# Value-scale squares, gate row and forget sums take other places in a hybrid attention layer

## The chip, the cores and the metric

The kernel runs on one core of a Trainium2 chip. The metric is the time of one execution on the device in microseconds (us). A run gives one time; where a median is named, it is over the runs shown. Engines are named PE (TensorE, with PEld for its weight loads), DVE (VectorE), ACT (ScalarE), POOL (GpSimd) and SP (SyncE, which here only issues DMAs). Line numbers with an L are those of the kernel before, unless the text says that they are of the changed one.

## What is computed

One residual sub-layer over 1024 tokens of width 1024, all in float32. The input is normalised and modulated (u), projected once to queries, keys, values and gates of 16 heads (and 8 columns for forget gates); eight heads do stick-breaking attention and eight do softmax attention with a cumulative forget gate; both are gated by SiLU, projected, multiplied by a modulation gate, added to the input and normalised. The reference, cut:

```python
mod = jax.nn.silu(c) @ w_ada[layer] + b_ada[layer]
shift, scale, gate = ...                       # three parts of 1024
u = layer_norm(x) * (1.0 + scale) + shift
fq, fk, fv, fg, ff, sq, sk, sv, sg = _split_columns(u @ w_in[layer])
log_f = log_sigmoid(ff + b_f)
f_cum = jnp.cumsum(log_f, axis=1)

# softmax heads
s = q @ k.T * scale + (f_q[..., :, None] - f_k[..., None, :])
p = softmax(where(causal, s, -inf));  out = p @ v

# stick-breaking heads
z = q @ k.T * scale
log_keep = where(strict, log_sigmoid(-z), 0.0)
later = cumsum(log_keep, axis=3, reverse=True) - log_keep
w = where(strict, exp(log_sigmoid(z) + later), 0.0);  out = w @ v

y = concat([y_fox * silu(fg), y_sb * silu(sg)]) @ w_out
x = layer_norm(DEEPNORM_ALPHA * x + gate * y, ln_g, ln_b)
```

Three small results matter here. The **value scales**: for pairs 2 to 7 the weights and values are kept as float16 parts, and the values are scaled by a factor that is worked out on the chip from the sum of squares of the value weights of their group. The **gate row**: gate = silu(c) @ w_ada, one row of 1024 numbers. The **forget sums**: the running sum of log_f over the 1024 tokens.

## The kernel before, in words

**Pairs and units.** Two heads share 128 partitions, so there are eight head pairs, four stick-breaking (0 to 3), then four softmax (4 to 7). A unit (p, h, i) is one block of 128 queries of head h of pair p against the i+1 blocks of keys up to it; there are 16 units to a pair, and `order(p)` says in which order. A step k of the main loop at the end of the program takes one unit's scores (`scores_turn`) and the weights of the unit two steps earlier for pairs 0 and 1, five steps earlier later (`weights_turn`).

**A stick-breaking unit** (`att_scores`, L598 on). PE computes the scores S into two PSUM banks (L611 and L613: high and low part of the keys). ACT reads them twice with a sigmoid: kp (L646) and be (L648). DVE runs a scan over kp from the right (L654, and L658 for the second half where the keys do not fit in 512 columns); in the program this is `tensor_tensor_scan`, and the order listing below names it SCALAR_TENSOR_TENSOR. POOL multiplies be by the scanned kp (L660). For pairs 0 and 1 PE then transposes the product in blocks of 128 into a PSUM buffer called T (L691, `att_transpose`); ACT copies it to the high part of pt and DVE subtracts to get the low part (L694), which frees the T buffer. There are two T buffers. Pairs 2 and 3 transpose by DMA instead. PE multiplies by the values into the "value bank" pv (`att_pv`, L720 for pairs 0 and 1, L709 later), whose columns 256 to 511 are idle for pairs 2 and on. ACT, DVE (L739, L740) and POOL (L741) turn it into a slice of y (tile ty).

**Projections as fillers.** Between the steps PE does matmuls of the later pairs' projections (L329 to L331 for q, k and g, L441 to L443 for values). They come from generators that are chained in `fillers`, near the end; each `yield` is one step, and `fill(want)` says how many steps stand behind each unit (52 in pair 0, 72 in pair 1). `beside(main, sides)` advances its side generators once with each step of its main one, and a `for _ in range(N): yield` in a side generator sets how many main steps it lets pass. The side generators are `gen_gate` (gate row), `gen_ranges` (value scales) and `gen_forget` (forget sums). Every weight is loaded by SP into one of two buffers (`raw_tile`, tag wraw) and split by POOL into a rounded high part (L144) and a low part (L145).

**The three side works before.** `gen_ranges` lets 18 steps pass, then loads 12 blocks of value weights (groups 1 to 3, four each, names n1_0 to n3_3) into the same two raw buffers and lets DVE square and sum each (L396, five steps apart); then PE transposes a column (u_row), and sums the 12 columns over partitions with a matmul by ones (ranges), and ten small DVE and POOL instructions (L402 to L420) make the six scales of the three groups. `gen_gate` starts the load of the bias bg, lets 20 steps pass, splits the two halves of the gate row on POOL (L968, L969) and sums them over partitions with two matmuls each (L978) and one DVE instruction each (L979) that reads PSUM. `gen_forget` works out the logarithms during pair 1 and 2, and then takes one turn of the two score buffers (`s_tile("f_ps", 2)`, L507) for two small matmuls (L509, L510), a copy by ACT, a transpose, another copy and a store.

**What sets the order.** PE's order is the order in which the program is written (`pe_order`). The order on DVE, ACT, POOL and SP is chosen by the tile scheduler from the program and its own estimates, so a piece that is written elsewhere may move others. Each engine runs its own queue strictly in order.

**PSUM.** Eight banks: two accumulators (acc), two pv banks, one score buffer S of two banks, and two further banks that are the two T buffers as long as transposes are done on PE, and a second score buffer from the first `s_tile(name, 2)` on (L81 to L85). From then on the scores alternate between the two.

## Time and profile before

| | |
|---|---|
| runs of the kernel before | 667.0, 666.96, 662.51 us, median 666.96 us |
| the profiled execution: its own time | 661.84 us |
| span of its instructions | 660.1 us, 10899 instructions |
| PE busy | 631.8 us, 96% of the span, 3558 matmuls and transposes |
| PE weight loads | 532.6 us, 81% |
| DVE busy | 517.8 us, 78%, 1011 instructions |
| ACT busy | 393.7 us, 60% |
| POOL busy | 352.4 us, 53% |
| DMA | 96.25 MB, 146 GB/s on average |

Reading it: a row of single instructions has the start, the length (both in us), the engine, the line, the operation with the tile it writes and the tile it reads, and in square brackets how long the engine was idle before it and which instruction ended that wait. A row of a group of instructions (one line or one tile) has the shortest, middle and longest duration in ns behind the count. A row of stretches has the length of the stretch, then the busy time (and number of instructions) of PE, PEld, DVE, ACT and POOL, then the granted TensorE clock as a share of full speed, the busy share of the DMA engines and GB/s. All starts are counted from the start of the span. Pair 0 lies at about 80 to 150 us, pair 1 at 147 to 225 us. In the profile the squares are named CUSTOM_DVE_ANT_0, and the scans TENSOR_TENSOR_SCAN.

### The profile page before, as it was taken

The page shows a single profiled execution, that of the slowest core. Times are in us where ns is not written, and L with a number is a line of the kernel's source. Part 1 is how long each engine was busy: PE and PEld are TensorE (multiplying, and loading weights), DVE is VectorE, ACT ScalarE, POOL GpSimd, SP SyncE. Part 2 cuts the span into 40 slices and gives each one's busy share as a digit, 9 for nine tenths or more (in the row PEclk, how much of TensorE's full clock was granted, in tenths as well). Part 3 has the DMA queues.
Part 4 walks back from the last instruction along what each step waited for, and adds up shares of the span by engine and source line. Part 5 has one row for each costly group of instructions (what it writes and reads, how often), then busy time and mean ns, then how long its engine had stood idle before and what let it go on. Part 6 is the DMA issues. An engine that isn't in the chain of part 4 may idle for free. (4 is left out here: it accounts for less than half of the span.)

```text
span 660.1 us, 10899 instructions
## 1 busy us (share of the span) xinstructions
PE 631.8 (96%) x3558; PEld 532.6 (81%) x3558; DVE 517.8 (78%) x1011; ACT 393.7 (60%) x825; POOL 352.4 (53%) x437
## 2 busy tenths in 40 slices
PE   8999988799999999999999999999999969999995
PEld 4889877688899877788998888889888758878884
DVE  6787879986867797978877685967678897996656
ACT  5577346675656867767867676767568866440000
POOL 5650177666635677778666333330534395775412
PEclk9999999899999999999999999999999998999999
DMA  9983543321210256747476666666595998895201
GB/s 324 402 313 130 171 123 110 106 58 37 55 29 15 65 115 114 165 112 156 104 178 155 166 141 157 133 155 113 128 184 135 247 258 190 204 220 182 86 33 64
DMA packets 153800, 96.25 MB, mean 146 GB/s; under 512 B 118224, under 2 KB 133136, under 8 KB 153744
## 3 DMA queue, kind: packets, MB, share of 16 engines
q1 hardware_dynamic: 152160, 91.09, 54.8%
q10 hardware_dynamic: 1584, 4.47, 2.1%
q8 instruction: 28, 0.46, 0.3%
q14 instruction: 28, 0.23, 0.1%
HBM read 55.13 MB, written 7.90 MB: 95 GB/s over the span
## 5 line engine op out<-in xcount | busy, mean ns | idle before, releaser
L329 PE MATMUL m<-uh,whi 128*128 128x512 f32 x304 | 123.0, 405 | 1.2 <-DVE kl L316 1.2
L331 PE MATMUL m<-uh,wlo 128*128 128x512 f32 x304 | 119.8, 394 | 0.0
L330 PE MATMUL m<-ul,whi 128*128 128x512 f32 x304 | 119.7, 394 | 0.0
L660 POOL TENSOR_TENSOR be<-be,kp 128x127 f32<-128x127 f32 (+3 forms) x64 | 90.0, 1406 | 45.0 <-DVE kp L658 25.5
L741 POOL TENSOR_TENSOR ty<-ty,sg 64x256 f32<-64x256 f32 x64 | 49.6, 775 | 91.8 <-DVE ty L736 52.5
L611 PE MATMUL S<-k,q 128*128 128x512 f32 (+4 forms) x192 | 68.5, 358 | 1.2 <-ACT be L648 1.0
L654 DVE TENSOR_TENSOR_SCAN kp<-kp,floor 128x128 f32<-128x128 f32 (+3 forms) x64 | 58.5, 913 | 14.3 <-ACT kp L646 13.6
L331 PEld LDWEIGHTS m<-uh,wlo 128*128 128x128 f32 x304 | 57.2, 188 | 13.6
L628 ACT ACTIVATE a<-a,nm 128x1024 f32<-128x1024 f32 (+7 forms) x64 | 49.7, 777 | 29.9 <-DVE nm L622 29.0
L329 PEld LDWEIGHTS m<-uh,whi 128*128 128x128 f32 x304 | 57.3, 188 | 12.0 <-PE m L331 1.2
L613 PE MATMUL S<-kl,qz 128*128 128x512 f32 (+4 forms) x192 | 65.7, 343 | 0.0
L330 PEld LDWEIGHTS m<-ul,whi 128*128 128x128 f32 x304 | 57.4, 189 | 9.7
L638 DVE SCALAR_TENSOR_TENSOR home<-a,l,home 128x1024 f16<-128x1024 f32 (+7 forms) x64 | 61.4, 959 | 4.2 <-ACT home L634 4.0
L622 DVE CUSTOM_DVE_ANT_0 a<-S,fb 128x1024 f32<-128x1024 f32 (+7 forms) x64 | 48.1, 751 | 18.9 <-PE S L613 15.7
L709 PE MATMUL pv<-home,v_g 128*128 128x256 f16 x480 | 56.3, 265 | 5.5 <-DVE ty L736 5.5
L709 PEld LDWEIGHTS <-v_g 128*128 128x128 f16 x480 | 44.2, 99 | 20.1 <-issue 14.3
L634 ACT ACTIVATE home<-a,l 128x1024 f16<-128x1024 f32 (+7 forms) x64 | 49.0, 772 | 15.2 <-DVE l L630 6.4
L646 ACT ACTIVATE kp<-S 128x384 f32<-128x384 f32 (+4 forms) x96 | 43.7, 491 | 23.6 <-PE S L613 21.8
L441 PE MATMUL v<-whi_v,uh 128*128 128x256 f32 (+1 forms) x192 | 54.7, 285 | 0.0
L443 PE MATMUL v<-wlo_v,uh 128*128 128x256 f32 (+1 forms) x192 | 54.4, 283 | 0.0
L442 PE MATMUL v<-whi_v,ul 128*128 128x256 f32 (+1 forms) x192 | 54.1, 282 | 0.0
L145 POOL TENSOR_TENSOR wlo<-raw,whi 128x512 fp32r<-128x512 f32 x38 | 50.9, 1343 | 2.0
(328 smaller groups left out, 1610.4 us busy)
## 6 DMA issues: line engine op xcount, KB each, us to landing
raw<-in_w_qkg_dram SPq DMA_DIRECT2D x38, 256.0 KB, 2.8
wss<-in_w_ss_dram SPq DMA_DIRECT2D x14, 512.0 KB, 8.2
x<-in_x_dram SPq DMA_DIRECT2D x8, 512.0 KB, 7.0
k<-k SPq DMA_DIRECT2D x32, 128.0 KB, 2.3
wg<-in_w_gate_dram SPq DMA_DIRECT2D x8, 512.0 KB, 4.3
fb<-f_dr ACTq DMA_DIRECT2D x8, 512.0 KB, 4.0
wor<-in_w_out_dram SPq DMA_DIRECT2D x8, 512.0 KB, 4.9
xr<-in_x_dram SPq DMA_DIRECT2D x8, 512.0 KB, 4.8
```

The lines of the kernel that those rows point to most:

```text
L329: nc.tensor.matmul(acc, hi[:, c], u_hi[kt][:, s], start=(kt == 0), stop=False)
L330: nc.tensor.matmul(acc, hi[:, c], u_lo[kt][:, s], start=False, stop=False)
L331: nc.tensor.matmul(acc, lo[:, c], u_hi[kt][:, s], start=False, stop=(kt == NB - 1))
L441: nc.tensor.matmul(acc[:, :n], u_hi[kt][:, ts_], hi[:, s], start=(kt == 0), stop=False)
L442: nc.tensor.matmul(acc[:, :n], u_lo[kt][:, ts_], hi[:, s], start=False, stop=False)
L443: nc.tensor.matmul(acc[:, :n], u_hi[kt][:, ts_], lo[:, s], start=False, stop=(kt == NB - 1))
L611: nc.tensor.matmul(S[:, s, :w], qst[p][h][:, qs], kst[p][h][:, ks], start=True, stop=False)
L613: nc.tensor.matmul(S[:, s, :w], z, klo[p][:, ks], start=False, stop=not masked)
L638: lows[:] = [nc.vector.scalar_tensor_tensor(lo, ab, l, hi, op0=ALU.mult, op1=ALU.subtract)]
L654: last_dve = nc.vector.tensor_tensor_scan(rv, rv, floor[:, :ke - lo], initial=0.0, op0=ALU.mult, op1=ALU.max)
L660: nc.gpsimd.tensor_tensor(be[:, :ke - 1], be[:, :ke - 1], kp[:, 1:ke], op=ALU.mult)
L709: nc.tensor.matmul(acc[:, q0:256], vt[p][:, kb, h * P:(h + 1) * P], pt[:, 2 * kb + x_, q0:], start=(kb == 0 and x_ == 0), stop=(kb == last ...
```

## The change

Three parts.

1. **Value scales.** The 12 squares are split. The four of group 1 come as before, and directly behind them the column transpose, the range matmul and the scales of group 1 alone. Then 20 further steps pass (NORM_LATE), then come the eight squares of groups 2 and 3, five steps apart, a second small matmul (ranges_late) and the scales of groups 2 and 3.
2. **Gate row.** 92 instead of 20 steps pass before the splits, the load of bg comes after them, and six instead of four steps lie behind each split. The value projection of group 1 (`gen_v(1)`) moves into the `beside` so that its steps still advance the two generators.
3. **Forget sums.** They no longer take a turn of the score buffers. Two functions (`sums`, `rows`) are put in a list, and `att_pv` runs the next of them at the end of a value product of pairs 2 and on, in the idle columns 256 to 511 of that product's own bank.

```diff
--- before.py
+++ after.py
@@ -95,9 +95,10 @@
     FGATE = 7
     FLOG = 8
     FROW = 16
-    GATE = 20
+    GATE = 92
     NORM_SPACE = 5
     NORM_AT = 18
+    NORM_LATE = 20
 
     def after(*instructions):
         stack = ExitStack()
@@ -387,7 +388,8 @@
                                 axis=mybir.AxisListType.X, apply_absolute_value=True)
         nc.vector.tensor_tensor(rng[:, 2:3], m2[:, 0:1], m2[:, 1:2], op=ALU.add)
         fr = modc.rearrange("p k i -> p (k i)")[:, :12]
-        for g in range(1, 4):
+
+        def squares(g):
             n = 528 if g == 1 else 512
             for h in range(4):
                 raw = raw_tile(f"n{g}_{h}")[:, :n]
@@ -397,6 +399,20 @@
                                                scalar=0.0, accum_out=fr[:, at:at + 1])
                 for _ in range(NORM_SPACE):
                     yield
+
+        def scales(g0, g1, norms):
+            up, down = rng[:, 4 + g0:4 + g1], rng[:, 7 + g0:7 + g1]
+            nc.vector.tensor_reduce(out=up, in_=norms.rearrange("p (g h) -> p g h", h=4), op=ALU.add,
+                                    axis=mybir.AxisListType.X)
+            nc.vector.tensor_scalar(up, up, 1.0e-30, None, op0=ALU.max)
+            nc.gpsimd.tensor_tensor(up, up, mhalf.to_broadcast([P, g1 - g0]), op=ALU.pow)
+            nc.gpsimd.tensor_scalar(up, up, top, 900.0, op0=ALU.mult, op1=ALU.mult)
+            nc.vector.reciprocal(down, up)
+            nc.vector.tensor_scalar(down, down, 1.0 / UP, None, op0=ALU.mult)
+            for g in range(g0, g1):
+                v_up[g], v_down[g] = up[:, g - g0:g - g0 + 1], down[:, g - g0:g - g0 + 1]
+
+        yield from squares(1)
         row = t_tile("u_row")[0:1, :P]
         nc.tensor.transpose(row, rng[:, 2:3], ident)
         nc.vector.tensor_reduce(out=rng[0:1, 3:4], in_=row, op=ALU.max, axis=mybir.AxisListType.X)
@@ -406,20 +422,18 @@
         yield
         ps_r = t_tile("ranges")
         nc.tensor.matmul(ps_r[:, 0:1], ones[0:1, :].to_broadcast([1, P]), rng[0:1, 3:4], start=True, stop=True)
-        nc.tensor.matmul(ps_r[:, 4:16], ones.to_broadcast([P, P]), fr, start=True, stop=True)
+        nc.tensor.matmul(ps_r[:, 4:8], ones.to_broadcast([P, P]), fr[:, :4], start=True, stop=True)
         top = rng[:, 4:5]
         nc.vector.tensor_scalar(top, ps_r[:, 0:1], 1.0e-30, None, op0=ALU.max)
         nc.vector.reciprocal(top, top)
-        up, down = rng[:, 5:8], rng[:, 8:11]
-        nc.vector.tensor_reduce(out=up, in_=ps_r[:, 4:16].rearrange("p (g h) -> p g h", h=4), op=ALU.add,
-                                axis=mybir.AxisListType.X)
-        nc.vector.tensor_scalar(up, up, 1.0e-30, None, op0=ALU.max)
-        nc.gpsimd.tensor_tensor(up, up, mhalf.to_broadcast([P, 3]), op=ALU.pow)
-        nc.gpsimd.tensor_scalar(up, up, top, 900.0, op0=ALU.mult, op1=ALU.mult)
-        nc.vector.reciprocal(down, up)
-        nc.vector.tensor_scalar(down, down, 1.0 / UP, None, op0=ALU.mult)
-        for g in range(1, 4):
-            v_up[g], v_down[g] = up[:, g - 1:g], down[:, g - 1:g]
+        scales(1, 2, ps_r[:, 4:8])
+        for _ in range(NORM_LATE):
+            yield
+        yield from squares(2)
+        yield from squares(3)
+        ps_r = t_tile("ranges_late")
+        nc.tensor.matmul(ps_r[:, :8], ones.to_broadcast([P, P]), fr[:, 4:12], start=True, stop=True)
+        scales(2, 4, ps_r[:, :8])
 
     rng = bss_sb.rearrange("p k i -> p (k i)")
 
@@ -504,20 +518,24 @@
                                 channel_multiplier=-1, compare_op=ALU.is_ge, fill=0.0)
         for _ in range(8):
             yield
-        f_ps = s_tile("f_ps", 2)
-        fp = f_ps[:, 0, :64]
-        nc.tensor.matmul(fp, tri, lf, start=True, stop=False)
-        nc.tensor.matmul(fp, ones.to_broadcast([P, P]), pre, start=False, stop=True)
         fc = cp.tile([P, 64], F32, tag="fab", name="fc")
-        nc.scalar.activation(fc, fp, AF.Copy, scale=-1.0)
+
+        def sums(room):
+            fp = room[:, :64]
+            nc.tensor.matmul(fp, tri, lf, start=True, stop=False)
+            nc.tensor.matmul(fp, ones.to_broadcast([P, P]), pre, start=False, stop=True)
+            nc.scalar.activation(fc, fp, AF.Copy, scale=-1.0)
+
+        def rows(room):
+            ft = room[:64, :P]
+            nc.tensor.transpose(ft, fc, ident)
+            nc.scalar.copy(fr, ft)
+            nc.sync.dma_start(f_dr.rearrange("h (t p) -> (h t) p", p=P), fr)
+
+        riders.extend((sums, rows))
         yield
-        yield
-        ft = f_ps[:64, 1, :P]
-        nc.tensor.transpose(ft, fc, ident)
-        nc.scalar.copy(fr, ft)
-        nc.sync.dma_start(f_dr.rearrange("h (t p) -> (h t) p", p=P), fr)
-        yield
-
+
+    riders = []
     fb = {}
 
     def load_fb(hh):
@@ -708,6 +726,8 @@
                 for x_ in range(2):
                     nc.tensor.matmul(acc[:, q0:256], vt[p][:, kb, h * P:(h + 1) * P], pt[:, 2 * kb + x_, q0:],
                                      start=(kb == 0 and x_ == 0), stop=(kb == last and x_ == 1))
+            if riders:
+                riders.pop(0)(acc[:, 256:])
             if p < 4:
                 summed.append((acc, p, h, j))
             else:
@@ -957,10 +977,10 @@
                                            op0=ALU.mult, op1=ALU.add)
 
     def gen_gate():
+        for _ in range(GATE):
+            yield
         b = att_tile("bg")
         nc.sync.dma_start(b, b_gate.to_broadcast([P, D]))
-        for _ in range(GATE):
-            yield
         parts = []
         for h in range(2):
             s = slice(h * 512, h * 512 + 512)
@@ -968,7 +988,7 @@
             nc.gpsimd.tensor_scalar(hi, gate[:, s], 1.0, 1.0, op0=ALU.mult, op1=ALU.mult)
             nc.gpsimd.tensor_tensor(lo, gate[:, s], hi.bitcast(F32), op=ALU.subtract)
             parts.append((hi, lo))
-            for _ in range(4):
+            for _ in range(6):
                 yield
         for h in range(2):
             s = slice(h * 512, h * 512 + 512)
@@ -1211,9 +1231,8 @@
             yield
 
     fillers = chain([
-        beside(chain([gen_rest(), gen_v(0, v0_w, range(4, NB)), gen_m(1, 2), gen_m(2, 0), gen_m(2, 1)]),
+        beside(chain([gen_rest(), gen_v(0, v0_w, range(4, NB)), gen_m(1, 2), gen_m(2, 0), gen_m(2, 1), gen_v(1)]),
                gen_gate(), gen_ranges()),
-        gen_v(1),
         beside(chain([gen_m(2, 2), gen_m(3, 0), gen_m(3, 1), gen_m(3, 2)]), gen_forget()),
         gen_m(4, 0), gen_m(4, 1), gen_v(2),
         gen_m(4, 2), gen_m(5, 0), gen_m(5, 1), gen_m(5, 2),
```

**DVE around the scans of units (0,1,4) and (0,1,5), pair 0.** Names are written with the unit (kp_0_1_4 is kp of unit (0,1,4)); n3_0 to n3_3 are the blocks of group 3 that are squared. `ISA` on an n tile is a square, and `ISA` on modc alone puts its sum in place. Line numbers are those of each program. Before:

```order
L654 SCALAR_TENSOR_TENSOR kp_0_1_4_1433<-kp_0_1_4_1433,floor_873 128x320
L658 SCALAR_TENSOR_TENSOR kp_0_1_4_1433<-kp_0_1_4_1433,floor_873 128x320
L396 ISA n3_3_1795,modc_142<-n3_3_1795 128x512
L396 ISA modc_142 128x1
L739 TENSOR_TENSOR ty_0_0_2_1442<-pv_0_0_2_1414,ty_0_0_2_1442 64x256
L740 TENSOR_TENSOR ty_0_0_2_1442<-pv_0_0_2_1414,ty_0_0_2_1442 64x256
L694 TENSOR_TENSOR pt_0_0_3_0_1406<-T_0_0_7_0_1459,pt_0_0_3_0_1406 128x4x128
L694 TENSOR_TENSOR pt_0_0_3_1_1421<-T_0_0_7_1_1466,pt_0_0_3_1_1421 128x4x128
L654 SCALAR_TENSOR_TENSOR kp_0_1_5_1478<-kp_0_1_5_1478,floor_873 128x384
L658 SCALAR_TENSOR_TENSOR kp_0_1_5_1478<-kp_0_1_5_1478,floor_873 128x384
```

Now, the same stretch:

```order
L672 SCALAR_TENSOR_TENSOR kp_0_1_4_1423<-kp_0_1_4_1423,floor_873 128x320
L676 SCALAR_TENSOR_TENSOR kp_0_1_4_1423<-kp_0_1_4_1423,floor_873 128x320
L410 RECIPROCAL bss_sb_101<-bss_sb_101 128x1
L759 TENSOR_TENSOR ty_0_0_2_1432<-pv_0_0_2_1404,ty_0_0_2_1432 64x256
L411 TENSOR_SCALAR bss_sb_101<-bss_sb_101 128x1
L398 ISA n3_0_1869,modc_142<-n3_0_1869 128x512
L398 ISA modc_142 128x1
L760 TENSOR_TENSOR ty_0_0_2_1432<-pv_0_0_2_1404,ty_0_0_2_1432 64x256
L712 TENSOR_TENSOR pt_0_0_3_0_1396<-T_0_0_7_0_1449,pt_0_0_3_0_1396 128x4x128
L712 TENSOR_TENSOR pt_0_0_3_1_1411<-T_0_0_7_1_1456,pt_0_0_3_1_1411 128x4x128
L672 SCALAR_TENSOR_TENSOR kp_0_1_5_1468<-kp_0_1_5_1468,floor_873 128x384
L398 ISA n3_1_1932,modc_142<-n3_1_1932 128x512
```

Behind the last row comes the second scan of unit (0,1,5). The last square of all (n3_3) stood here before; now n3_0 stands nearly at its place, n3_1 between the two scans, and n3_2 and n3_3 come in pair 1, after the scans of unit (1,0,4). The other four (n2_0 to n2_3) stand earlier in pair 0 than this stretch, behind the scan of (0,0,3), the second scan of (0,0,4) and the copies of (0,0,5) and (0,0,6).

**POOL around the gate's splits.** Before, in pair 0, between the splits of value weights and the first be products:

```order
L968 TENSOR_SCALAR whi_gate_0_1021<-gate_91 128x512
L145 TENSOR_TENSOR wlo_v0_3b_863<-raw_v0_3b_860,whi_v0_3b_862 128x512
L661 MEMSET be_0_0_1_930 128x1
L660 TENSOR_TENSOR be_0_0_1_930<-be_0_0_1_930,kp_0_0_1_929 128x255
L969 TENSOR_TENSOR wlo_gate_0_1022<-gate_91,whi_gate_0_1021 128x512
L968 TENSOR_SCALAR whi_gate_1_1107<-gate_91 128x512
L661 MEMSET be_0_0_2_958 128x1
L660 TENSOR_TENSOR be_0_0_2_958<-be_0_0_2_958,kp_0_0_2_957 128x383
L969 TENSOR_TENSOR wlo_gate_1_1108<-gate_91,whi_gate_1_1107 128x512
```

Now the second half stands in pair 1, behind the product of unit (1,1,2); L408 and L409 are the power and the product of the scales of groups 2 and 3:

```order
L678 TENSOR_TENSOR be_1_1_2_2172<-be_1_1_2_2172,kp_1_1_2_2171 128x383
L408 TENSOR_TENSOR bss_sb_101<-bss_sb_101,mhalf_92 128x2
L761 TENSOR_TENSOR ty_1_0_3_2178<-ty_1_0_3_2178,sg_1_1286 64x256
L988 TENSOR_SCALAR whi_gate_1_2128<-gate_91 128x512
L409 TENSOR_SCALAR bss_sb_101<-bss_sb_101 128x2
L989 TENSOR_TENSOR wlo_gate_1_2129<-gate_91,whi_gate_1_2128 128x512
L679 MEMSET be_1_1_3_2235 128x1
L145 TENSOR_SCALAR whi_2_2_0_2456<-raw_2_2_0_2454 128x512
L678 TENSOR_TENSOR be_1_1_3_2235<-be_1_1_3_2235,kp_1_1_3_2234 128x511
```

On PE the matmuls of the second half (gate_1) stand behind the scores of unit (1,1,3) and the first six matmuls of v_1_4, the value projection of one block of tokens.

**PE around the forget sums, at the turn from pair 1 to pair 2.** pv_2_0_3 is the first value product of pair 2, S_2_0_0 the scores of a unit of pair 2. Before (v_g1 rows cut), the two matmuls of the sums write a score buffer, f_ps, ahead of the value product:

```order
L331 MATMUL m_3_0_1_2755<-uh_3_129,wlo_3_0_0_2664 128x512
L509 MATMUL f_ps_2768<-flf_144,fscratch_2708 128x64
L510 MATMUL f_ps_2768<-fsb_143,ones_79 128x64
L709 LDWEIGHTS v_g1_2010
L709 MATMUL pv_2_0_3_2773<-home_0_2596,v_g1_2010 128x256
```

Now they stand behind it and write its own bank, ahead of the scores:

```order
L727 MATMUL pv_2_0_3_2777<-home_0_2604,v_g1_1986 128x128
L525 MATMUL pv_2_0_3_2777<-flf_144,fscratch_2716 128x64
L526 MATMUL pv_2_0_3_2777<-fsb_143,ones_79 128x64
L629 MATMUL S_2_0_0_2797<-k_2_0_1766,q_2_0_1577 128x128
L631 MATMUL S_2_0_0_2797<-kl_2_1768,qz00_83 128x128
```

Since f_ps took one turn of the two score buffers, S_2_0_0 and all scores behind it now take the other buffer than before.

## The prediction

> **What bounds the kernel now.** I read the page first, for the share of each engine, then who waits on TensorE (PE), then the stretches of the first pairs, then single rows there.
>
> ```profile
> PE 631.8 (96%) x3558; PEld 532.6 (81%) x3558; DVE 517.8 (78%) x1011; ACT 393.7 (60%) x825; POOL 352.4 (53%) x437
> ```
>
> PE is busy for 631.8 of 660.1 us. The change removes hardly any PE work, so the most that it can win is part of the 28.3 us in which PE stands still. The waits of PE name the places:
>
> ```profile
> PE T L691 <- DVE pt L694: 3.5, 1, 3.5
> PE gate L978 <- DVE gate L979: 1.6, 1, 1.6
> PE pv L720 <- DVE pt L694: 1.5, 1, 1.5
> PE S L611 <- ACT be L648: 1.0, 1, 1.0
> PE v L441 <- DVE kl L316: 1.0, 1, 1.0
> PE T L691 <- POOL be L660: 0.9, 1, 0.9
> ```
>
> The columns are total, number of waits and the longest. Five of the six (all but the fourth) lie in pair 0, between 82 and 132 us, and sum to 8.5 us. Four of them end on VectorE (DVE), and the fifth on a GpSimd (POOL) product that a DVE scan releases. The stretches show the same:
>
> ```profile
> 99.00:115.00 16.00, 13.68 (x93) 12.25 (x91) 15.27 (x33) 10.98 (x31) 11.10 (x15) 1.00 0.37 103
> 127.00:132.00 5.00, 4.88 (x20) 4.40 (x21) 4.86 (x8) 1.75 (x5) 3.59 (x4) 0.66 0.45 120
> 132.00:148.00 16.00, 16.00 (x87) 13.35 (x86) 13.66 (x22) 11.88 (x26) 10.92 (x14) 1.00 0.22 60
> 181.00:198.00 17.00, 17.00 (x131) 16.38 (x130) 11.25 (x28) 9.59 (x26) 6.81 (x12) 1.00 0.13 33
> ```
>
> After the length come PE, PEld, DVE, ACT and POOL busy, then the clock. From 99 us DVE is the full engine (15.27 of 16) and PE the waiting one. From 132 us PE is full, and DVE is idle for 6 of 17 us by 181 us. So DVE work that goes from pair 0 to pair 1 is worth something, and PE work that goes there costs its whole length. In 127 to 132 us the granted clock is 0.66: 5.0 x 0.34 = 1.7 us lost behind the wait of 3.5.
>
> **The change on DVE in pair 0.** The order of instructions says that of the eight squares only two (n3_2, n3_3) really leave pair 0. The other six stay, at other places. What one costs:
>
> ```profile
> L396 DVE CUSTOM_DVE_ANT_0 n<-n x12: 656/677/1687, 86.8 to 133.7; 128x512 f32<-128x512 f32 x8, 128x528 f32<-128x528 f32 x4
> DMA to landing us min/median/max: 2.5/2.7/3.8
> 90.96 1.51 DVE L396 CUSTOM_DVE_ANT_0 n<-n 128x528 f32<-128x528 f32 x1 [1.01 <-DMA n<-in_w_vf_dram]
> 109.67 0.66 DVE L396 CUSTOM_DVE_ANT_0 n<-n 128x512 f32<-128x512 f32 x1
> 110.26 0.07 DVE L396 DVE_READ_ACCUMULATOR2_ANT modc<- 128x1 f32 x1
> 109.82 1.46 POOL L660 TENSOR_TENSOR be<-be,kp 128x511 f32<-128x511 f32 x1 [0.43 <-DVE kp L654]
> 163.41 1.09 POOL L660 TENSOR_TENSOR be<-be,kp 128x511 f32<-128x511 f32 x1 [0.21 <-DVE kp L654]
> 120.00 0.69 DVE L396 CUSTOM_DVE_ANT_0 n<-n 128x512 f32<-128x512 f32 x1 [1.14 <-DMA n<-in_w_v_dram]
> 123.43 2.27 POOL L660 TENSOR_TENSOR be<-be,kp 128x895 f32<-128x895 f32 x1 [3.60 <-DVE kp L658]
> 124.56 1.69 DVE L396 CUSTOM_DVE_ANT_0 n<-n 128x512 f32<-128x512 f32 x1
> 127.12 0.63 PE L691 MATMUL T<-ident,be 128*128 128x128 f32 x4 [3.47 <-DVE pt L694]
> ```
>
> The shortest square takes 0.66 us plus 0.07 for its sum, the longest 1.69. The long one at 124.56 began inside POOL's product of 123.43 and ended 0.55 us after it (126.25 against 125.70): it stood still until POOL was done. The one at 109.67 began 0.15 us ahead of POOL's product and took 0.66, and the product took 1.46 where the same product alone takes 1.09. So whichever starts second waits for the other. The Trainium skill says this on the page "SBUF — State Buffer", in "Who interferes with whom": a VectorE instruction with two SBUF inputs and a GpSimd instruction that reads SBUF block each other entirely. The trace agrees (1.69 against 0.66), and the rule speaks against the new places. The last row is the costliest wait: the square of 1.69 stands ahead of the copy (pt) that frees a transpose buffer, and PE waits 3.47 us for that copy.
>
> I add up what DVE gains ahead of its last critical scan in pair 0, the second 384-wide scan of unit (0,1,5):
>
> ```profile
> 137.29 1.01 DVE L658 TENSOR_TENSOR_SCAN kp<-kp,floor 128x384 f32<-128x384 f32 x1
> 138.38 1.54 POOL L660 TENSOR_TENSOR be<-be,kp 128x767 f32<-128x767 f32 x1 [0.16 <-DVE kp L658]
> 141.69 0.81 PE L691 MATMUL T<-ident,be 128*128 128x128 f32 x6
> 107.08 0.67 DVE L979 SCALAR_TENSOR_TENSOR gate<-bg,gate 128x512 f32<-128x512 f32 x1
> 167.51 0.27 DVE L402 TENSOR_REDUCE bss_sb<-u_row 1x1 f32<-1x128 f32 x1
> 171.99 0.16 DVE L414 TENSOR_REDUCE bss_sb<-ranges 128x3 f32<-128x12 f32 x1
> 86.78 1.37 DVE L396 CUSTOM_DVE_ANT_0 n<-n 128x528 f32<-128x528 f32 x1 [1.04 <-DMA n<-in_w_vf_dram]
> 116.25 0.89 DVE L396 CUSTOM_DVE_ANT_0 n<-n 128x512 f32<-128x512 f32 x1
> ```
>
> - two squares gone: 2 x 0.74 = 1.5 won
> - two gate sums gone: 2 x 0.67 = 1.3 won
> - seven small instructions of the first scale come in: 0.27 and six at up to 0.16, 1.2 lost
> - waits for a square's data: 1.01 + 1.14 = 2.15 now. A load can only start when an earlier user has freed one of two buffers and takes 2.7 to land; the last four squares form such a chain, so I keep 1.5 of it: 0.65 won
> - standing still behind POOL: now 0.70, 0.84, 0.22 and 1.02 above 0.67, in all 2.8. In the new order n2_0, n2_1 and n3_0 stand one to three short instructions behind the scan that releases POOL's product, so the product begins first. They lose what is left of it: 1.09 - 0.29, 1.32 - 0.43 and 1.32 - 0.73, in all 2.3 (1.32 is estimated for 639 columns, between 1.09 for 511 and 1.54 for 767; the short ones between are estimated at 0.15 to 0.3 each, from the small rows above). The other three meet weight splits, about 0.4 each. In all 3.5: 0.7 lost
>
> The sum is 1.5 + 1.3 - 1.2 + 0.65 - 0.7 = 1.6 us. In the trace the product is done at 139.92 and PE needs it at 141.69, so there are 1.8 us of slack: PE can arrive 1.6 + 1.8 = **3.4 us earlier** at this transpose. It has more than that to win ahead of it (8.5 us of waits, 1.7 of clock), so DVE sets this figure, and the clock loss is not added again. The Trainium skill's page "TensorE: Matmul & The Clock Gate", Part 1, says that PE falls to half its clock after an idle window of about 3.4 us; the 0.66 behind the 3.47 agrees, and with no wait of that length left the stretch should go. That it adds nothing here is because DVE decides afterwards.
>
> Bounds: if all six squares stand still for a whole product of about 1.3 us, 7.8 instead of 3.5, the lead is -0.9; if none stands still and no data is late, 3.5 + 1.5 more, 8.4.
>
> **The gate in pair 1.** Four gate matmuls leave pair 0, where their time is part of the slack, and enter pair 1, where PE is full:
>
> ```profile
> 103.73 0.39 PE L978 MATMUL gate<-wlo_gate,half 128*128 128x512 f32 x1
> 103.97 0.28 PE L441 MATMUL v<-whi_v_3b,uh 128*128 128x256 f32 x1
> 195.23 0.86 POOL L660 TENSOR_TENSOR be<-be,kp 128x383 f32<-128x383 f32 x1 [0.53 <-DVE kp L654]
> 173.36 0.88 POOL L417 TENSOR_TENSOR bss_sb<-bss_sb,mhalf 128x3 f32<-128x3 f32 x1
> 196.05 0.72 POOL L741 TENSOR_TENSOR ty<-ty,sg 64x256 f32<-64x256 f32 x1
> 179.70 0.62 POOL L144 TENSOR_SCALAR whi<-raw 128x512 fp32r<-128x512 f32 x1
> L969 POOL TENSOR_TENSOR wlo_gate<-gate,whi_gate x2: 1287/1292/1298, 86.3 to 90.6; 128x512 fp32r<-128x512 f32 x2
> 196.79 0.40 PE L613 MATMUL S<-kl,qz 128*128 128x512 f32 x1
> ```
>
> From start to start one takes 0.24 (103.73 to 103.97), four 0.94: a **loss of 0.9**. The second half also has a new wait. POOL now runs, behind the product of 195.23, the power (0.88), a ty product (0.72), the gate's high part (0.62, as any split of 512), a short scaling (0.3, as the reduce of 167.51) and its low part (1.29), and ends at 196.1 + 3.8 = 199.9. On PE the matmul of the low part stands behind the scores of 196.79 (done with 0.24 later), the two gate matmuls of the first half (0.5), six value matmuls of half their width (6 x 0.12) and the high part (0.24): about 198.6. Queued behind it are the value matmuls of all that follows, so PE waits up to 1.3; I take **1.0 lost**, bounds 0 and 1.3. The splits that stand behind it on POOL are of pair 2's weights, and the product behind those waits for a scan that POOL reaches early (0.53 idle ahead of 195.23, row above). The load of bg now stands on SyncE's queue ahead of a copy of keys that only pair 2 reads. The two late squares fall where DVE idles a third of the time: nothing.
>
> **The forget sums.** Before, they take one turn of the two score buffers, so that the next scores get the buffer that was used last:
>
> ```profile
> 245.75 0.58 ACT L648 ACTIVATE be<-S 128x512 f32<-128x512 f32 x1
> 246.38 0.33 PE L611 MATMUL S<-k,q 128*128 128x128 f32 x1 [1.01 <-ACT be L648]
> ```
>
> PE waits 1.01 us until ScalarE has read it. With the sums in the value bank, these scores take the other buffer, which has been free for long. The same three matmuls and two copies remain; the copies now sit in the bank that the next value product needs, but stand ahead of that product's own last reader. Bounds 0.4 (DVE is close to full there, so part may come back) and 1.0; I take **0.8 won**.
>
> **Sum:** -3.4 + 0.9 + 1.0 - 0.8 = -2.3. Against the profiled execution (661.84 us, span 660.1) that is **659.5 us**. The runs shown are 667.0, 666.96 and 662.51: with the profiled one, two near 667 and two near 662, 5 us apart, and nothing in one profile tells why. The forecast stands on the lower level; the median, 666.96, is on the upper one, where the same saving gives 664.7.
>
> **Rivals.** (1) *The squares hardly stand still*, because their later places let POOL finish first: the lead is 8.4, less 0.9, plus 1.0, with no gate wait at most 8.5; with half of the blocking 6.3 won, 655.5 us. For it: the 3.47 and 1.7 us surely depend on one square that leaves its place. Against it: three squares stand right behind the scans that start POOL. (2) *DVE comes out no earlier*: the six squares that stay eat what two squares and two sums free. Then PE wins the 1.8 of slack and 0.4 to 0.8, and pays 1.9: 661.4 us, no change. (3) *Slower*: the gate's low part is late by more than a product. It decides if POOL reaches the split later than 3.4 us after PE asks, which needs a further product (1.1) and a split pair (1.9) ahead of it; PE then waits 4.2 and loses 1.7 of clock as at 127 us, and with a DVE lead of 0: 661.84 - 1.8 + 0.9 + 5.9 - 0.8 = 666.0. POOL's idle 10 of 17 us there speak against it.
>
> **How the numbers follow.** Forecast 0.42, rival 1 0.24, rival 2 0.24, rival 3 0.10. A measurement of this kernel tells about 1% (6.6 us) from no change. Faster by more: rival 1 in most cases, and a part of the forecast if before is measured on its upper level: 0.34. Slower by more: a part of rival 3, or the change on the upper level: 0.07. Within 1%: 0.59. The range reaches from rival 1 with a little more, 654.5, to the forecast and rival 2 on the upper level, 666.5; the forecast's own range is 657 to 662.
>
> **What would show it.** PE's wait of 3.47 us at the transposes of unit (0,0,6) and the clock of 0.66 are gone, replaced by several waits of 0.3 to 1.5 us in pair 0. Six squares run in pair 0, at least three of them over 1.2 us. The transpose of unit (0,1,5) comes near 138.3 us. In pair 1 PE waits about 1 us at the gate's second low part. The wait of scores on ScalarE's be is gone. I am wrong if squares run at 0.7 us and PE has no waits in pair 0 (rival 1), or if PE waits in pair 1 for squares or the gate by more than 2 us.

## The result and the profile after

The changed kernel takes 659.16 us (median of 15 runs, 657.63 to 663.47) against 665.56 us of the kernel before (15 runs, 661.22 to 667.04); the ratio is 0.9938, with a 95% interval from 0.9917 to 0.996. Its profiled execution took 660.06 us, 1.8 us less than that of before (661.84). The forecast was 659.5. One run of before, taken beside a later kernel (701.12 us), and one of the kernel with eight steps below (1036.85 us), in which the granted clock was 0.85 and 0.56, are left out of all medians, ratios and intervals.

The two medians are 6.4 us apart, where 2.3 were forecast. The forecast subtracts 2.3 from a profiled execution of before that lies near the lower end of its runs, while nine of its 15 runs here took 664.71 us or more, and nine of the 15 runs of the changed kernel took 660.06 or less. Beside the later kernels the median of before was 662.5 to 662.6 us. That 659.16 lies so close to 659.5 is therefore partly luck. What the change itself saves is read from the two profiled executions, row by row.

The page's busy times hardly move. PE is busy as long as before, and what is won is waiting:

```profile
PE 632.3 (96%) x3560; PEld 532.2 (81%) x3560; DVE 517.3 (79%) x1015; ACT 393.5 (60%) x825; POOL 350.9 (53%) x439
```

The waits of PE, in the changed kernel (total, number, longest):

```profile
PE T L709 <- DVE pt L712: 2.2, 4, 1.2
PE T L709 <- POOL be L678: 1.7, 3, 0.9
PE v L455 <- DVE kl L317: 1.2, 1, 1.2
PE gate L998 <- POOL be L679: 0.9, 1, 0.9
PE pv L740 <- DVE pt L712: 0.4, 1, 0.4
PE ranges L424 <- DVE pt L712: 0.3, 1, 0.3
```

The single wait of 3.5 us on pt has become four that sum to 2.2 (0.28, 0.17 and 1.25 in pair 0, 0.46 in pair 1), the gate's wait has moved to pair 1, and the wait of scores on be is gone. The stretches of pair 0 show PE fuller and still waiting towards the end (lengths, then PE, PEld, DVE, ACT, POOL, clock):

```profile
99.00:115.00 16.00, 15.01 (x107) 13.78 (x106) 14.11 (x28) 12.41 (x34) 13.76 (x18) 1.00 0.40 115
127.00:132.00 5.00, 4.83 (x26) 3.64 (x24) 4.71 (x9) 3.99 (x9) 3.08 (x5) 1.00 0.18 52
132.00:148.00 16.00, 13.96 (x73) 11.26 (x73) 14.28 (x25) 8.95 (x20) 11.60 (x15) 1.00 0.27 76
181.00:198.00 17.00, 15.80 (x117) 14.72 (x116) 12.50 (x33) 8.32 (x23) 9.02 (x16) 1.00 0.04 9
```

DVE is still the engine that sets pair 0 (14.28 of 16 us from 132 us), and pair 1, where PE had no wait in the profile before, has 1.2 us of idle PE between 181 and 198 us.

To see where time is won and lost, I follow certain scores from kernel to kernel. The rows of PE that compute them, before:

```profile
83.12 0.28 PE L611 MATMUL S<-k,q 128*128 128x256 f32 x1
147.59 0.31 PE L611 MATMUL S<-k,q 128*128 128x128 f32 x1
178.04 0.48 PE L611 MATMUL S<-k,q 128*128 128x512 f32 x1
201.64 0.31 PE L611 MATMUL S<-k,q 128*128 128x320 f32 x1
239.75 0.39 PE L611 MATMUL S<-k,q 128*128 128x512 f32 x1
253.35 0.45 PE L611 MATMUL S<-k,q 128*128 128x448 f32 x1
```

and in the changed kernel:

```profile
83.30 0.28 PE L629 MATMUL S<-k,q 128*128 128x256 f32 x1
144.69 0.31 PE L629 MATMUL S<-k,q 128*128 128x128 f32 x1
174.40 0.50 PE L629 MATMUL S<-k,q 128*128 128x512 f32 x1
201.46 0.31 PE L629 MATMUL S<-k,q 128*128 128x320 f32 x1
239.59 0.39 PE L629 MATMUL S<-k,q 128*128 128x512 f32 x1
251.75 0.46 PE L629 MATMUL S<-k,q 128*128 128x448 f32 x1
```

They are the scores of units (0,0,1), (1,0,0), (1,0,7), (1,1,4), (2,0,3) and (2,1,6). I call the stretches between them pair 0, 1a, 1b, 1c and the turn to pair 2. The expectations below count the same rows as steps: step 1, 24, 34, 41, 57 and 60. Differences from row to row give:

| stretch, us | before | after | difference |
|---|---|---|---|
| pair 0 (step 1 to 24) | 64.47 | 61.39 | -3.08 |
| 1a (24 to 34) | 30.45 | 29.71 | -0.74 |
| 1b (34 to 41) | 23.60 | 27.06 | +3.46 |
| 1c (41 to 57) | 38.11 | 38.13 | +0.02 |
| turn to pair 2 (57 to 60) | 13.60 | 12.16 | -1.44 |

The sum is -1.78, and the two profiles differ by 1.78. So the kernel is 3.8 us ahead when it enters 1b, gives back nearly all of it there, and keeps what the forget sums bring.

### The profile page after: what moved, and what is told of

Its sections match the earlier page's. It is cut to its first block, busy times and chain, and to the rows that moved or that the text cites. A ratio compares the mean times of both kernels' runs of the same rounds, so it can differ in the third digit from the quotient of the medians.

```text
span 658.3 us, 10902 instructions
## 1 busy us (share of the span) xinstructions
PE 632.3 (96%) x3560; PEld 532.2 (81%) x3560; DVE 517.3 (79%) x1015; ACT 393.5 (60%) x825; POOL 350.9 (53%) x439
```

## The experiments

**One part at a time, and all but the gate.** Four kernels: each of the three parts alone on the kernel before, and the changed kernel with the gate row put back.

```diff
 forget_only:  + riders.extend((sums, rows)); riders.pop(0)(acc[:, 256:]) in att_pv   (nothing else)
 gate_only:    + GATE = 92, bg loaded behind the yields, 6 yields; gen_v(1) inside beside
 squares_only: + squares split, scales of group 1 early; gen_v(1) inside beside
 no_gate:      the changed kernel with GATE = 20, bg loaded first, 4 yields
```

> The kernel before with the third part alone (forget sums in the value bank). Theory (the parts are separate, each worth what the two traces show in its place): pairs 0 and 1 as before; at the turn to pair 2 the wait of 1.01 us of the scores on be is gone and the profile is 1.2 to 1.5 us shorter from there to the end. Rival (what is won there comes back, since DVE is nearly full from 232 to 250 us): 0 to 0.4 us shorter at the end. Timed against before: ratio 0.998 by the theory, 0.9995 or more by the rival.

> The kernel before with the gate row's part alone (92 steps, sums and matmuls in pair 1; all eight squares stay where they were). Theory: pair 0 gets the wait of 1.57 us on the gate's sum, four matmuls (0.94 us) and two DVE sums (1.34 us) back, but keeps the square of 1.69 us and a wait over 2 us behind it; pair 1 pays 0.94 us of matmuls and a wait of about 0.9 us. In all within 1.5 us of before, to either side. Rival (the lead of pair 0 in the changed kernel comes from the gate row, not from the squares): pair 0 ends 3 us or more earlier here too, and the whole is 1 us or more shorter.

> The kernel before with the value scales' part alone (squares split; gate row in pair 0 and forget sums as before). Theory (squares and their standing still behind POOL make the lead of pair 0, and the gate row pays it back in pair 1): the wait of 3.47 us is gone, pair 0 ends 1.5 to 3 us earlier, and pair 1 gives back less than 0.8 us, so the whole is 1 to 3 us shorter. Rival (it is the gate's leaving that frees DVE): pair 0 ends less than 1 us earlier, the whole within 0.7 us of before.

> The changed kernel with the gate row put back into pair 0 (20 steps), squares and forget sums as changed. Theory: the gate row costs pair 1 2.1 us (0.94 of matmuls, 0.88 of wait, the rest of copies) and frees pair 0 of less, since DVE's two sums and POOL's splits lie partly in waits there; so this kernel is 0 to 1.5 us shorter than the changed one (profile from 656.8 to 658.3 us). Rival (the gate row in pair 0 brings its wait of 1.57 us and DVE's 1.34 us back in full): 1 to 2.5 us longer than the changed kernel.

Measured, with the stretches read as above:

| | median us | ratio to before, 95% | pair 0 | 1a | 1b | 1c | turn |
|---|---|---|---|---|---|---|---|
| forget sums alone | 661.22 | 0.9995 (0.9961 to 1.0028) | 65.35 | 30.46 | 23.60 | 38.11 | 12.32 |
| gate row alone | 665.66 | 1.0035 (1.0005 to 1.0064) | 65.01 | 30.47 | 24.99 | 38.12 | 13.58 |
| squares alone | 658.79 | 0.9948 (0.9922 to 0.9974) | 61.42 | 29.74 | 24.63 | 38.12 | 13.60 |
| all but the gate | 657.44 | 0.9934 (0.9904 to 0.9964) | 63.38 | 29.80 | 24.65 | 38.10 | 12.33 |

The forget sums do what the theory says in their place: the turn takes 12.32 instead of 13.60 us and the wait on be is gone. Their ratio can't be told from 1, since 1.3 us is less than the interval; it is the 0.9995 that the rival named, and the interval holds the theory's 0.998 too. The profile as a whole is not shorter, because the part behind the turn is 5.05 us longer there, with a wait of 2.41 us that before does not have. The gate row alone makes the kernel slower, by 1.85 us in its profile (663.69), a little more than the theory allowed. It frees pair 0 of the wait of 1.57 us, but PE then meets the next long one, which is longer than before. Behind it the granted clock from 126 to 133 us is 0.51, 3.4 us lost, where before loses 1.7; so 1.7 us of this profile's pair 0 are the longer stretch of half clock. Single waits of that kernel's PE:

```profile
118.70 0.85 PE L691 MATMUL T<-ident,be 128*128 128x128 f32 x6 [0.75 <-DVE pt L694]
126.75 1.09 PE L691 MATMUL T<-ident,be 128*128 128x128 f32 x4 [4.17 <-DVE pt L694]
```

The squares alone win the 3.05 us of pair 0 without the gate row, so their rival (it is the gate's leaving that frees DVE) fell. 1.7 of the 3.05 us is the half clock that stood behind the wait of 3.47: from 127 to 132 us the clock is 1.00 here, 0.66 before. All but the gate is as fast as the changed kernel or a little faster; the intervals overlap, so from the times alone the gate's price stays open. Its profiled execution ran at a mean granted clock of 0.937, where all other profiles here have 0.985 to 0.996, so I take its time from the runs and read only 1b and the turn from its stretches.

**Where the gate's 2.4 us go.** 1b takes 24.63 us with the squares alone and 27.06 with the gate row as well. One kernel gave the gate's matmuls more room behind its splits:

```diff
-            for _ in range(6):
+            for _ in range(8):
                 yield
```

> The changed kernel with eight instead of six steps behind each of the gate's splits. Theory: PE's wait of 0.88 us for the gate's low part in pair 1 is gone or under 0.2 us, and the stretch from the scores of step 34 to those of step 41 takes 26.2 us instead of 27.06; the rest as in the changed kernel. Rival (PE and POOL are both late there for another reason): the wait moves along and stays over 0.5 us.

It takes 658.48 us (ratio 0.9911, 0.9879 to 0.9943), but not for the reason expected: 1b takes 27.07 us and the wait stays at 0.86. Here the rival held, and the rows of POOL say why. In the changed kernel:

```profile
192.74 0.87 POOL L678 TENSOR_TENSOR be<-be,kp 128x383 f32<-128x383 f32 x1 [0.53 <-DVE bss_sb L405]
193.71 0.72 POOL L408 TENSOR_TENSOR bss_sb<-bss_sb,mhalf 128x2 f32<-128x2 f32 x1
194.40 0.73 POOL L761 TENSOR_TENSOR ty<-ty,sg 64x256 f32<-64x256 f32 x1
195.10 0.61 POOL L988 TENSOR_SCALAR whi_gate<-gate 128x512 fp32r<-128x512 f32 x1
195.93 1.27 POOL L989 TENSOR_TENSOR wlo_gate<-gate,whi_gate 128x512 fp32r<-128x512 f32 x1
```

and with eight steps:

```profile
195.27 1.09 POOL L678 TENSOR_TENSOR be<-be,kp 128x511 f32<-128x511 f32 x1 [0.80 <-DVE bss_sb L411]
196.33 0.62 POOL L988 TENSOR_SCALAR whi_gate<-gate 128x512 fp32r<-128x512 f32 x1
197.03 1.27 POOL L989 TENSOR_TENSOR wlo_gate<-gate,whi_gate 128x512 fp32r<-128x512 f32 x1
```

The scheduler moved the split behind one more product (195.27), so the matmul that came later still meets it late. PE's row of the wait shows it at 198.35 instead of 197.25:

```profile
198.35 0.49 PE L998 MATMUL gate<-wlo_gate,half 128*128 128x512 f32 x1 [0.86 <-POOL wlo_gate L989]
```

What this kernel gained over the changed one in its profile lies in pair 0 (59.73 against 61.39 us), in an order that is nearly the same; the point on the clock, further down, tells what differs. The gate's account is then: the stretch of pair 0 is 1.7 us shorter with the gate row gone (59.73 against 61.42 with the squares alone; both without a stretch of half clock), and 1b is 2.43 us longer, of which 0.88 is the wait, 1.2 the four matmuls, and the rest goes with a wait of 0.46 us for a copy. With the gate row alone the same matmuls meet a wait of only 0.19 us, and 1b is 1.39 us longer. A loss of 0.7 us by the profiles, too small for the times to show.

**What the six squares cost that stayed.** In the changed kernel six of eight late squares still run in pair 0. From the kernel that is all but the gate, two were made: one holds the late squares on DVE behind the copies that stand ahead of them in the program, so that all eight run in pair 1; one leaves the eight squares and their loads out and sets their sums to a constant. A third holds them and also puts the column transpose and the range sums off.

```diff
 pin:          + with after(*lows[-1:]):            # groups 2 and 3 only; lows[-1] is the last pt copy (DVE)
                     nc.vector.tensor_tensor_reduce(out=raw, in0=raw, in1=raw, ...)
 no_squares:   - yield from squares(2); yield from squares(3)
               + nc.vector.memset(fr[:, 4:12], 100.0)   and 40 yields
 late_row_pin: pin, with 34 yields ahead of u_row instead of 20 behind scales(1, 2), late squares 3 apart
```

> Squares and forget sums as changed, gate row in pair 0 as before, and the eight late squares held on DVE behind the pt copy that stands ahead of them in the program, so that all eight really run in pair 1 (in the changed kernel six of them stay in pair 0). Theory (the squares that stay cost pair 0 what they take and stand still): against the same kernel without the hold, the two waits of the last transposes on pt (0.75 and 0.52 us) are gone, and the stretch from the first scores to those of step 24 takes 59 to 60.2 us, against 61.4 with the squares alone changed. Rival (the stretch is set by other work, such as the column transpose and the range sums that came into pair 0): 61.0 us or more. Pair 1 as it was, within 0.5 us.

> Squares and forget sums as changed, gate row in pair 0 as before, and the eight late squares and their loads left out (their sums are set to a constant, so the scales of groups 2 and 3 are not the reference's). Theory: pair 0 is as short as with the squares held in pair 1 (59 to 60.2 us to step 24) and pair 1 no more than 0.3 us shorter, since they meet idle time there. Rival: the loads of the squares hold back loads of weights, and this kernel is over 1 us shorter than the one with the hold.

> As the kernel with the late squares held in pair 1, and the column transpose, the range sums and the scale of group 1 also go to pair 1, 34 steps later, with three steps instead of five between the late squares. In pair 0 PE waited 0.42 us for the buffer of the column, 0.94 us for DVE to read it, and 0.68 us for the buffer of the sums, 2.04 us in all. Theory: these go, and pair 0 takes 1 to 2 us less than with the hold alone, while pair 1 gets 0.7 us of PE work back: 0.3 to 1.3 us shorter. Rival (the waits are DVE's lateness, and show at the next transpose instead): pair 0 no shorter, the whole 0.5 to 1 us longer.

| | median us | ratio to before, 95% | pair 0 | 1a | 1b | 1c | turn |
|---|---|---|---|---|---|---|---|
| late squares held in pair 1 | 660.53 | 0.9942 (0.9917 to 0.9967) | 57.85 | 29.61 | 29.90 | 38.10 | 12.35 |
| late squares left out | 653.58 | 0.9835 (0.9806 to 0.9863) | 57.85 | 29.61 | 23.81 | 38.09 | 12.30 |
| held, column and sums later | 662.07 | 0.9985 (0.9958 to 1.0011) | 56.77 | 30.43 | 30.87 | 38.11 | 12.23 |

Pair 0 is as short with the squares held as without them: 57.85 us, 3.6 less than with six of them there (61.42). More than I had expected (59 to 60.2). But with the hold 1b takes 6.1 us more than without squares, where I had expected no more than 0.5, and the rival of the second expectation held. 4.0 of the 6.1 are two waits; behind them the granted clock from 174 to 181 us is 0.76, 1.7 us lost. The waits of the kernel with the hold, on PE:

```profile
PE v L458 <- POOL wlo_v L146: 2.1, 1, 2.1
PE v L456 <- POOL whi_v L145: 1.9, 1, 1.9
```

PE waits for the split of the weights of value group 1. On POOL the split waits for its load, and the load was started late. POOL's row in that kernel:

```profile
168.53 0.63 POOL L145 TENSOR_SCALAR whi_v<-raw_v 128x528 fp32r<-128x528 f32 x1 [1.00 <-DMA raw_v<-in_w_vf_dram]
```

and SyncE's queue of issues around it, where n is a square's block and raw_v a value weight:

```profile
156.66 3.94 SPq L396 DMA_DIRECT2D n<-in_w_v_dram  x3
164.54 0.45 SPq L771 DMA_DIRECT2D y_dr<-ty  x1
165.05 0.58 SPq L141 DMA_DIRECT2D raw_v<-in_w_vf_dram  x1
```

Without the squares the four loads of raw_v start between 118.4 and 150.7 us, here between 165.0 and 177.0. The squares' loads take turns with them in the two raw buffers, and a square that is held keeps its buffer. The third kernel won 1.1 us more in pair 0 by taking the column and the sums away, as its theory said, and lost 1.8 in pair 1. As a whole it is longer, as its rival had it, but for another reason: pair 0 did get shorter.

**Is it the buffers?** Two more kernels, both with the gate row in pair 0: one holds the squares as above but loads them into the six att buffers (of kp and be); the other puts the late squares' loads behind those of value group 1, with their sums over partitions in the value bank.

```diff
 pin_att:      - raw = raw_tile(f"n{g}_{h}")[:, :n]
               + raw = (raw_tile if g == 1 else att_tile)(f"n{g}_{h}")[:, :n]
 late_squares: squares(2), squares(3) run beside gen_m(2, 2) .. gen_m(3, 2), 3 yields apart;
               - ps_r = t_tile("ranges_late")
               + riders.append(late_sums)          # the same matmul and scales in acc[:, 256:]
```

> The kernel with the eight late squares held in pair 1, but these squares are loaded into the six att buffers (where kp and be live) instead of the two raw buffers. Theory (the raw buffers are what made PE wait 1.90 and 2.10 us for the split of v1's weights): these two waits are gone, and steps 34 to 41 take 23.8 to 25 us instead of 29.9. Rival (POOL is late there by itself, or DVE by the squares): over 28 us, with waits on whi_v and wlo_v as before.

> Forget sums as changed, gate row in pair 0 as before, and the loads of the eight late squares put behind the loads of value group 1 and of pair 2's first gate weights; their sums over partitions go through the value bank in pair 2. Theory (with the hold in pair 1 PE waited 4.0 us because the squares kept the two raw buffers from the weights of value group 1, and nothing else is paid there): no wait over 0.6 us from 145 to 205 us, steps 1 to 24 in 57.5 to 58.3 us and steps 34 to 41 in 23.6 to 24.3 us; profile 653 to 655 us, ratio 0.983 to 0.988. Rival (the same happens to the weights of pair 3): waits of 2 us or more between 205 and 260 us, ratio over 0.990.

With the att buffers the kernel takes 655.18 us (ratio 0.9902, 0.9869 to 0.9936); 1b takes 24.90 us instead of 29.90 and both waits are gone, with them the half clock (1.00 in all five stretches). So it was the buffers. The later loads give 655.79 us (0.9896, 0.9857 to 0.9936), 1b 24.32 us. That ratio is above what the theory gave. 1c has a wait of 0.80 us behind a square of 2.42, and the turn, where the sums of the late squares now go through the value bank, takes 13.32 us with a wait of 0.83; both are under the 2 us of the rival. Its profile also has 6.8 us of half clock in pair 0, from 95.5 us (59.95 us instead of 57.85), behind waits of 1.47 and 1.01 us. Both kernels compute the whole layer. Against their own runs of before they stand at 0.990, the changed kernel at 0.9938; the intervals overlap a little, and by the profiled executions with no such stretch in pair 0 the first is 2.85 us shorter (655.35 against 658.20 of the changed kernel with eight steps).

**Do squares stand still because of their second operand?** In the changed kernel, each late square was replaced by a sum of absolute values of the same block, which reads one SBUF operand. The order on DVE is the same.

```diff
-                nc.vector.tensor_tensor_reduce(out=raw, in0=raw, in1=raw, op0=ALU.mult, op1=ALU.add, ...)
+                nc.vector.tensor_reduce(out=fr[:, at:at + 1], in_=raw, op=ALU.add, axis=X,
+                                        apply_absolute_value=True)          # groups 2 and 3
```

> The changed kernel with each of the eight late squares replaced by a sum of absolute values of the same block, which reads one operand from SBUF instead of two and writes only the sum (the scales of groups 2 and 3 are then other numbers); the order on every engine is otherwise that of the changed kernel. Theory (the squares stand still behind POOL because of their second SBUF operand): none of the six in pair 0 takes over 0.8 us, where four took 0.87 to 1.41, and PE waits 1.5 to 2.5 us less up to step 24 than in the changed kernel (5.36). Rival (they are long for another reason, such as data or POOL writing): two or more stay over 1.2 us, and the waits within 0.5 us of 5.36.

Three squares of the changed kernel in pair 0:

```profile
121.30 1.26 DVE L398 CUSTOM_DVE_ANT_0 n<-n 128x512 f32<-128x512 f32 x1
126.63 1.41 DVE L398 CUSTOM_DVE_ANT_0 n<-n 128x512 f32<-128x512 f32 x1
130.84 1.35 DVE L398 CUSTOM_DVE_ANT_0 n<-n 128x512 f32<-128x512 f32 x1 [0.18 <-DMA n<-in_w_v_dram]
```

and POOL at the same places:

```profile
121.29 0.72 POOL L761 TENSOR_TENSOR ty<-ty,sg 64x256 f32<-64x256 f32 x1
125.50 2.00 POOL L678 TENSOR_TENSOR be<-be,kp 128x1023 f32<-128x1023 f32 x1 [3.09 <-DVE bss_sb L407]
130.32 1.32 POOL L678 TENSOR_TENSOR be<-be,kp 128x639 f32<-128x639 f32 x1 [1.46 <-DVE bss_sb L410]
```

POOL's instructions end at 122.01, 127.50 and 131.64; the squares end at 122.56, 128.04 and 132.19. Each ends 0.54 or 0.55 us after POOL, as the one of 1.69 us did before. The group of the sums with one operand, from the kernel that has them:

```profile
L402 DVE TENSOR_REDUCE modc<-n x8: 664/686/686, 106.8 to 163.0; 128x1 f32<-128x512 f32 x8
```

All eight take 0.66 to 0.69 us, also the three that start inside a POOL instruction (at 124.59, 128.04 and 131.36; the first lies in a product of 123.46 to 125.46). PE's waits in pair 0 fall from 5.36 us (the sum over its rows) to 3.28, and pair 0 takes 57.59 us; of the 3.8 us to the changed kernel 1.7 are a stretch of half clock that this profile doesn't have (see the point on the clock below). The time is 655.92 us (ratio 0.9895, 0.9864 to 0.9927). The theory held on each count, the rival fell. One thing more differs, though: a square also writes its block back to SBUF, the sum does not. A row of the changed kernel shows that the write is not the cause:

```profile
126.03 0.69 DVE L712 TENSOR_TENSOR pt<-T,pt 128x512 fp32r<-128x512 f32 x1
```

T lies in PSUM, so this copy reads one SBUF operand; it writes 128x512 to SBUF, lies wholly inside POOL's product of 125.50 to 127.50, and takes its 0.69 us. The square right behind it takes 1.41. The rule of the Trainium skill on the page "SBUF — State Buffer", section "Who interferes with whom", which the prediction cited, is thereby shown for this case: 1.26 to 1.41 us with two operands against 0.68 to 0.69 with one, at the same places of the order.

## Why the prediction was right, point by point

- **DVE's lead in pair 0.** The forecast was that DVE is 1.6 us ahead at the second scan of unit (0,1,5), and PE 3.4 at its transposes. In the changed kernel:

```profile
135.78 1.00 DVE L676 TENSOR_TENSOR_SCAN kp<-kp,floor 128x384 f32<-128x384 f32 x1
138.46 0.87 PE L709 MATMUL T<-ident,be 128*128 128x128 f32 x6 [0.48 <-POOL be L678]
```

  The scan starts 1.5 us earlier (137.29 before) and the transposes 3.2 us (141.69 before). The single terms were less good than their sum. Standing still behind POOL came to 2.8 us, as long as before, not 3.5. The six squares stand still for 2.2 (0, 0.02, 0.59, 0.74, 0.68 and 0.20 above 0.67). The first two, n2_0 and n2_1, were to lose 0.80 and 0.89 because POOL's product begins first; they began within 0.03 us of it or ahead of it, and it was the products that took longer (1.65 and 1.73 us, against 1.09 and 1.32). The first four squares, which the forecast left out of the new sum, still stand still for 0.6, less than before (0.71 us where it was 1.37, 1.15 where it was 1.51): POOL no longer splits the gate row there. With the squares alone changed these two keep 1.43 each. Waiting for a square's data (all but the first) took 0.93 us, not 1.5. And the 1.3 us of the two gate sums are not a term of their own: with the gate row alone PE's long wait became 4.17 instead of 3.47 us. Only once the squares had gone from that place did the gate row's leaving bring 1.7.
- **The wait of 3.47 us** went, and behind 120 us six of 0.17 to 1.25 us came in its place in pair 0, as foreseen. Three squares over 1.2 us in pair 0, as foreseen.
- **The clock.** The step "with no wait of that length left the stretch should go" failed for the profiled run. The stretch of half clock went from 127 us, and another stands behind the waits of 0.45 and 1.21 us at 92.6 and 95.4:

```profile
91.00:99.00 8.00, 6.34 (x39) 5.88 (x38) 6.93 (x15) 3.32 (x9) 4.51 (x9) 0.79 0.47 135
```

  0.21 of 8 us is 1.7 us. In the kernel with eight steps the same place has waits of 0.39 and 1.45 us and a clock of 1.00:

```profile
91.00:99.00 8.00, 6.17 (x50) 5.71 (x48) 7.34 (x16) 4.37 (x12) 4.28 (x6) 1.00 0.46 129
```

  Its pair 0 is 1.66 us shorter, just the price of that stretch. The price reaches DVE. In the changed kernel it waits for a copy that comes late behind the slowed PE:

```profile
99.69 0.69 DVE L712 TENSOR_TENSOR pt<-T,pt 128x512 fp32r<-128x512 f32 x1 [1.53 <-ACT pt L711]
```

  and with eight steps hardly, so that the scan and the transposes of unit (0,1,5) come 1.64 us earlier still:

```profile
98.47 0.69 DVE L712 TENSOR_TENSOR pt<-T,pt 128x512 fp32r<-128x512 f32 x1 [0.20 <-ACT pt L711]
134.14 1.00 DVE L676 TENSOR_TENSOR_SCAN kp<-kp,floor 128x384 f32<-128x384 f32 x1
136.82 0.87 PE L709 MATMUL T<-ident,be 128*128 128x128 f32 x6 [0.49 <-POOL be L678]
```

  So the reason given for leaving the clock out of the sum, that DVE decides afterwards, does not hold for a stretch that early. In that kernel, without the stretch, the scan leads by 3.15 us where 1.6 was forecast, and the transposes by 4.87 where 3.4 was. The forecast lead was about 1.5 us too small, and a clock loss that it had not foreseen made up for it: its size came out right by luck. The rows show only that such a stretch comes with some executions and not with others (of the two kernels under "Is it the buffers?", with waits of 1.47 or 1.48 and 1.01 us here, one has 6.8 us of half clock behind them and the other none), behind waits much shorter than the 3.4 us of the rule cited from the Trainium skill; what decides was not tried.
- **The gate in pair 1** was forecast to cost 0.9 and 1.0. Its wait is 0.88, and the matmuls take 1.20: 0.47 the first two, and 0.73 the second two, which stand on both sides of the wait. What failed as an account of pair 1 is the rest of 1b. It lost 3.46 in all, 1.6 more than forecast. 1.0 of this is there without the gate (24.63 against 23.60 us): a wait for a transpose and the late range sums (0.33 and 0.14), and slower issue that I can't put down to one row. I had costed the late squares in pair 1 at nothing; with them left out 1b takes 23.81 us instead of 24.65, so most of it is theirs. The gate adds the 0.26 by which its matmuls took longer, and a wait of 0.46 for a copy. Against that stands a gain I had left out: the column transpose and the range sums leave 1a, 0.74.
- **The forget sums** were sized at 0.8, bounds 0.4 and 1.0. They brought 1.28 alone and 1.44 in the changed kernel, more than the upper bound: the wait of 1.01, and less PE time besides. The reason given for less than 1.0, that DVE is nearly full there, did not show: nothing came back up to step 60.
- **The two rivals of size.** Rival 1 (the squares hardly stand still) gave 655.5 us. In the changed kernel they do stand still; when the second operand of the late ones was taken away, it took 655.92, so the rival had the worth of it about right. Its reason, that POOL would be done first, did not come. Rival 3 (the gate over 2 us late) didn't come: 0.88.

By the stretches the sum was then -3.08 - 0.74 + 3.46 + 0.02 - 1.44 = -1.8 where -2.3 was forecast. Pair 1 cost 0.84 more than forecast and pair 0 gave 0.32 less; the forget sums gave 0.64 more. So the mechanism was right in its direction in all three places, and its sizes were helped by errors that cancelled.

## What to carry to other kernels

Moving work in the program moves it on the chip only if something holds it: six of eight squares stayed, and only a hold on DVE moved them (my reading, not tried apart, is that their loads were early and the scheduler took the first idle place); look at the order on the engine before pricing the move. A piece that waits with a buffer in its hand delays whoever needs that buffer next, so a hold that won 3.6 us in one stage lost 6.1 in the next until it had buffers of its own. And where DVE and GpSimd share a stage, count the SBUF operands: one instead of two took 2.1 us of waits out of one stage.

## What the runs showed of the hardware that was not expected

- A square, with its two operands, that has to stand still behind a POOL instruction ends 0.54 or 0.55 us after it in the four cases above (126.25 after 125.70 before; 122.56, 128.04 and 132.19). In all the profiles here every square that starts at least 0.2 us inside a POOL instruction of more than one column ends 0.53 to 0.57 us after it, or 0.65 and 0.66 where it started in the last 0.05 us. Alone it takes 0.67, so it is as if it made only about 0.1 us of progress until POOL is done. Where both start within 0.2 us of each other either can lose: the square of 108.02 began 0.03 us behind a product and took 0.67, and the product took 1.65 instead of 1.09; the one of 121.30 began 0.01 behind and took 1.26.
- The spread of the times is explained only in part. The kernel without late squares took 653.03 to 654.17 us in five runs; the one with the att buffers, whose profile has no wait of PE over 1.5 us in pairs 0 and 1 either, took 654.56 to 660.91 in eight. So the length of the waits there does not decide it. The granted clock of each run is on record. Of 19 runs of before that were taken together, twelve took 661.29 to 663.22 us at a mean clock of 0.9911, and seven took 665.42 to 667.07 at 0.9889. The clock is worth 0.0022 x 662 = 1.5 us of the 3.9 us between the two groups. The rest stays open.
- What follows one and the same wait differs. The forget sums alone leave pair 0 as it was, with a wait of 3.44 us where before has 3.47. The stretch behind it in the profile of before (length, PE, PEld, DVE, ACT, POOL, clock):

```profile
115.00:132.00 17.00, 13.14 (x61) 10.92 (x62) 15.56 (x27) 10.85 (x25) 11.28 (x12) 0.90 0.40 113
```

and with the forget sums alone:

```profile
115.00:132.00 17.00, 13.22 (x59) 11.03 (x60) 15.44 (x26) 10.12 (x22) 11.31 (x12) 0.82 0.36 111
```

0.10 and 0.18 of 17 us are 1.7 and 3.1 us lost. Pair 0 is 0.88 us longer in the second. That is the smaller part of what lies between the two executions (666.49 and 661.84 us): 5.05 us come behind the turn to pair 2, where the second has one wait more, of 2.41 us, and a clock of 0.72 from 595 to 601 us, another 1.7 us.
